# Attention in an encoder block: value products directly behind the next unit's transposes in TensorE's order, the dense products behind them

## The chip, the cores and the metric

The kernel runs on one core of one Trainium2 chip. The metric is the device time of one execution in microseconds (us). Before the change it is 1884.78 us, the median of three runs (1884.11 to 1885.09 us).

## The reference

One layer of a bidirectional encoder runs over two request groups (2048 and 512 tokens, width 1024), each with 16 learned meta tokens in front. Cut to what matters:

```
u = rms_norm(h, norm_g)
qa, ka, va, za, qb, kb, vb, zb, ga, gb = split(u @ w_in)
o_a = neighbourhood_attention(qa, ka, va, na_rpb)   # 8 heads of 64, 8 x 16 token window, plus meta tokens
o_b = window_attention(qb, kb, vb, t5_bias, sink)   # 8 query heads, 2 key heads, +-128 tokens, meta tokens, sink
y_a = (o_a * silu(za)) @ w_proj_a
y_b = (o_b * silu(zb)) @ w_proj_b
h = h + (sigmoid(ga) * y_a + sigmoid(gb) * y_b) @ w_out
out = rms_norm(h without meta tokens, final_g)
```

All is fp32 in the reference. In the kernel an operand of a matmul is split into a high part (rounded to fp32r) and a low part (the rest), and a product is made of three matmuls, or two where one side is narrow.

## The kernel before, in words

The tokens are cut into five windows of 512 (`w` = 0 to 4). The first part (to about 960 us) makes the input projections and stores q, k, v, z and gates in DRAM. The second part, of which the change is a part, runs attention and the dense rest side by side. Its work is cut into 240 **units**. A window has 32 A units, one for each of 8 heads (`p`, `h`) and 4 column groups (`g`), and then 16 B units (`gh` = 0, 1; query block `n` = 0 to 3; `i` = 0, 1), each for two heads. A unit is a generator (`unit_a`, `unit_b`) with five stages:

1. load: q, k, v, bias by DMA, issued on SyncE (SP).
2. **scores** on TensorE (lines 1117 and 1118, or 1223 and 1224, into `s`), maximum with bias on VectorE (line 1047), exponential on ScalarE (line 1054).
3. normalise: reciprocal (line 1058) and scaling (line 1065 on VectorE, line 1063 on ScalarE).
4. **transposes** of the probabilities on TensorE into `tp` (line 1141, or 1243 and 1246), then the split into `ph` (high, ScalarE, line 1144 or 1250) and `pl` (low, VectorE, line 1145 or 1251). In B units the meta tokens go to `pms` by three small copies: lines 1260 (ScalarE), 1261 (VectorE) and 1262 (ScalarE).
5. **value products** on TensorE into `oa` or `ob` (lines 1156 and 1158, or 1267, 1270 and 1272), which read `ph`, `pl` and `pms`, then `ol` (ScalarE, line 1162 or 1274) and the sum into `y` (VectorE, line 1164 or 1277). Of an A head the column group 0 has no value products of its own; they run with those of group 1. The last unit of a pair of heads also multiplies by `z` (GpSimd) and splits the result for the dense part (line 1071 on ScalarE, 1072 on GpSimd).

The dense part (`phases`: gates, `dense_pa`, `dense_pb`, `dense_out`, `dense_fin`) is a generator too. One of its steps is six matmuls of 128x512 (`mm3` twice, lines 146 to 148). `fill(share)` adds `share` to a running sum and makes one step for each whole number reached: `share` is 1 for most B units and 0.5 for most A units, so a B unit has a dense step in each of its two fills and an A unit one in its second fill. In window 0 the shares differ a little, so that some fills make no step.

The loop at the end of `encoder_block` writes TensorE's order out by hand (`manual_schedule` for PE). In an iteration it makes the loads of unit i + 4, the scores of i + 2, the normalising of i + 1, a fill, the transposes of i, a second fill, and the value products of i - 1. The order of the other engines is set by a scheduler from a modelled timeline of the whole program, so it can shift when TensorE's order does. `ph` and `pl` are one tile each; A units write alternating parts of it, B units alternate between two halves. `oa` and `ob` have one PSUM buffer, `tp` has three, shared with a third of the A scores, `s` two, and the dense results two.

Of the kernel before, what the change touches and what calls it, by code (L numbers as in the profile page):

```python
# [95 lines left out]
def encoder_block(ctx: ExitStack, tc: tile.TileContext, xT, x_end, w_in, w_pa, w_pb, w_o, norm_g, final_g,  # L96
# [44 lines left out]
    def move(out, in_):  # L141
        last_move[0] = nc.sync.dma_start(*(f32(a) if a.dtype == F32R else a for a in (out, in_)))
        return last_move[0]
# [73 lines left out]
    class Weights:  # L217
# [16 lines left out]
        def next(self):  # L234
            i = self.i
            self.i += 1
            self.fetch(i + 2)
            self.split(i + 1)
            return self.wt.pop(i)
# [1256 lines left out]
    def phases(w, br):  # L1496

        if br == "a":
            if w == 0:
                yield from islice(gates, GATES_A)  # L1500
            else:
                yield from dense_pb(w - 1)
                yield from dense_out(w - 1, range(0, 4))
        elif w == 0:
            yield from gates
            open_dense()
            yield from dense_pa(0)
        else:
            yield from dense_out(w - 1, range(4, 8))
            pa = dense_pa(w)  # L1510
            yield from islice(pa, 1)
            yield from with_fill(pa, dense_fin(w - 1))
# [7 lines left out]
    units = []  # L1520
# [31 lines left out]
    with tc.manual_schedule(engines={E.PE}):  # L1552
        N = len(units)
        dense, key, due = iter(()), None, 0.0

        def fill(amount):
            nonlocal due
            due += amount
            while due >= 1 and next(dense, "end") != "end":
                due -= 1  # L1560

        for i in range(1, 4):
            next(units[i][2])
        for _ in islice(gates, GATES_0 - 4):
            pass
        for i in range(2):
            next(units[i][2])
        for _ in islice(gates, 4):
            pass
        vbm = vbm_d.rearrange("m g (h f) -> m g h f", h=2)  # L1570
        for h in range(2):
            for r, part in ((0, 0), (32, 0), (64, 1)):
                move(vms[r + 16 * h : r + 16 * h + 16, :, h], vbm[:, :, part, :])
        next(units[0][2])
        for i in range(N):
            br, w, _, weight = units[i]
            if key != (br, w):
                key, dense = (br, w), chain(dense, phases(w, br))
            if i == N - LAST:
                lo_eng[0] = nc.vector  # L1580
            share = COUNT.get(key, 32) * weight / 32 / 2
            if i + 4 < N:
                next(units[i + 4][2])
            if i + 2 < N:
                next(units[i + 2][2])
            if i + 1 < N:
                next(units[i + 1][2])
            fill(share)
            next(units[i][2])
            if [u[0] for u in units[i + 1 : i + 3]] == ["a", "b"]:  # L1590
                next(units[i + 2][2])
            fill(share)
            if i:
                next(units[i - 1][2])
        fill(2)
        next(units[N - 1][2])
        for _ in dense:
            pass
# [106 lines left out]
```

## Time and profile before

| what | us |
|---|---|
| median of three runs | 1884.78 |
| the profiled execution, its own time | 1881.95 |
| its span, first to last instruction | 1880.0 |
| VectorE busy in the span | 1326.6 |
| ScalarE busy in the span | 1146.9 |
| GpSimd busy in the span | 729.4 |

A row of a timeline has the start in us from the span's start, the duration in us, the engine (PE is TensorE, DVE VectorE, ACT ScalarE, POOL GpSimd), the line of the kernel, the operation, the tiles (out<-in), the shapes, and the count of merged instructions. Matmuls overlap in the pipeline, so the time from one start to the next is what a matmul costs TensorE, and the duration is longer than that. A row of the windows has the stretch, its length, and then the busy time of each engine with its count of instructions, the granted TensorE clock (1.00 is full) and the DMA load. A row of the waits names an engine and an instruction, what it waited for, the sum, how often, and the longest.

### The profile page before, as it was taken

Reading aid. Unit: us, or ns where it says so; the run is one execution under the profiler, and the core shown is the slowest. Engines: PE = TensorE matmul, PEld = TensorE weight load, DVE = VectorE, ACT = ScalarE, POOL = GpSimd, SP = SyncE. Lnnn points to the kernel's source line nnn. Section 1 sums busy time; section 2 is a strip of 40 time slices with the busy share of each in tenths; the row PEclk is TensorE's granted clock in tenths of the full one; section 3 lists DMA queues with packets and bytes.
Section 4 is the critical chain, followed back from the end, with each engine's and each line's share of the span. In section 5 each row is a group of like instructions: output and inputs, shape, how many; then the busy total and the mean of one; then the engine's idle time right before and its main releaser. Section 6 shows DMA issues by size and latency. Waiting matters only on the chain.

```text
span 1880.0 us, 29819 instructions
## 1 busy us (share of the span) xinstructions
PE 1857.8 (99%) x9797; PEld 1584.9 (84%) x9797; DVE 1326.6 (71%) x2961; ACT 1146.9 (61%) x2528; POOL 729.4 (39%) x558
## 2 busy tenths in 40 slices
PE   8999999999999999999999999999999999999998
PEld 6988888888888888888878888888888888888887
DVE  8885657556477565444457888878887887888874
ACT  6454444434465443444456797797889788878932
POOL 2005343222202322232323435656844764684420
PEclk9999999999999999999999999999999999999999
DMA  7575666555295677744359878977995996698473
GB/s 262 193 197 187 189 188 183 200 193 184 78 330 197 188 209 208 201 145 150 113 186 320 270 230 264 300 218 243 324 284 178 321 315 225 221 314 261 115 298 132
DMA packets 288145, 414.35 MB, mean 220 GB/s; under 512 B 117736, under 2 KB 162360, under 8 KB 286456
## 3 DMA queue, kind: packets, MB, share of 16 engines
q1 hardware_dynamic: 287704, 412.45, 68.4%
q8 instruction: 78, 1.28, 0.3%
q14 instruction: 75, 0.61, 0.1%
q10 hardware_dynamic: 288, 0.01, 0.0%
HBM read 303.46 MB, written 108.91 MB: 219 GB/s over the span
## 4 chain that ended last, share of the span: by engine, by line
PE 83%; ACT 5%; DVE 5%; DMA 4%; issue 1%; SPq 1%; POOL 1%; ACTq 0%; DVEq 0%
PE pa L850 23%; PE pe L850 11%; PE pc L850 6%; PE mm L148 3%; PE mm L147 3%; PE mm L146 3%; PE tp L1141 3%; PE pso L148 2%; PE psb L148 2%; PE pso L146 2%; PE psb L146 2%; PE pso L147 2%; PE psb L147 2%; PE psa L146 2%; PE psa L148 2%; PE psa L147 2%
## 5 line engine op out<-in xcount | busy, mean ns | idle before, releaser
L208 POOL TENSOR_TENSOR wt<-wraw,wt 128x512 fp32r<-128x512 f32 x164 | 213.0, 1317 | 270.0 <-ACT wt L207 269.9
L850 PE MATMUL pa<-u,wt 128*128 128x512 f32 x1008 | 244.3, 391 | 2.1 <-ACT wt L207 1.1
L850 PE MATMUL pa<-u,x 128*128 128x512 f32 x984 | 236.7, 389 | 0.5 <-ACT u L861 0.5
L850 PEld LDWEIGHTS pa<-u,wt 128*128 128x128 f32 x1008 | 189.9, 189 | 42.4 <-ACT wt L207 1.5
L207 ACT CAST wt<-wraw 128x512 fp32r<-128x512 f32 x312 | 177.9, 619 | 74.7 <-DMA wraw<-in_w_in_dram 27.4
L850 PEld LDWEIGHTS pa<-u,x 128*128 128x128 f32 x984 | 184.5, 188 | 39.3 <-ACT u L861 0.9
L821 POOL TENSOR_TENSOR s<-wraw,raw 128x512 f32<-128x512 f32 x40 | 58.2, 1456 | 278.8 <-DVE x L208 278.8
L146 PE MATMUL mm<-u,wt 128*128 128x512 f32 (+2 forms) x416 | 150.3, 361 | 7.0 <-ACT u L334 7.0
L816 POOL TENSOR_TENSOR s<-raw 128x512 f32<-128x512 f32 x40 | 58.7, 1467 | 234.7 <-DMA raw<-in_w_in_dram 233.2
L147 PE MATMUL mm<-u,wt 128*128 128x512 f32 (+2 forms) x416 | 146.8, 353 | 1.1 <-DVE u L335 1.0
L148 PE MATMUL mm<-u,wt 128*128 128x512 f32 (+2 forms) x416 | 146.8, 353 | 0.1
L208 DVE TENSOR_TENSOR wt<-wraw,wt 128x512 fp32r<-128x512 f32 x148 | 104.7, 745 | 53.8 <-ACT wt L207 53.7
L850 PE MATMUL pe<-u,wt 128*128 128x512 f32 x504 | 121.4, 390 | 0.0
L850 PE MATMUL pc<-u,wt 128*128 128x512 f32 x504 | 121.1, 389 | 0.0
L850 PE MATMUL pe<-u,x 128*128 128x512 f32 x480 | 115.3, 389 | 0.0
L850 PEld LDWEIGHTS pc<-u,wt 128*128 128x128 f32 x504 | 94.6, 188 | 19.6
L850 PEld LDWEIGHTS pe<-u,wt 128*128 128x128 f32 x504 | 94.4, 188 | 19.6
L1144 ACT CAST ph<-tp 128x384 fp32r<-128x384 f32 (+6 forms) x160 | 81.7, 511 | 44.9 <-PE tp L1141 43.5
L1047 DVE CUSTOM_DVE_ANT_0 s<-s,ba 128x384 f32<-128x384 f32 (+5 forms) x160 | 86.9, 544 | 30.6 <-PE s L1118 27.7
L1145 DVE TENSOR_TENSOR pl<-tp,ph 128x384 fp32r<-128x384 f32 (+6 forms) x160 | 94.9, 593 | 18.0 <-ACT ph L1144 15.2
L146 PE MATMUL pso<-mh,wt 128*128 128x512 f32 x256 | 107.1, 418 | 0.0
L829 POOL TENSOR_TENSOR s<-wraw,s 128x512 f32<-128x512 f32 x40 | 53.7, 1343 | 136.2 <-DVE wt L208 135.6
(258 smaller groups left out, 5030.1 us busy)
## 6 DMA issues: line engine op xcount, KB each, us to landing
wraw<-in_w_in_dram SPq DMA_DIRECT2D x86, 512.0 KB
raw<-in_w_in_dram SPq DMA_DIRECT2D x40, 512.0 KB
q<-qa SPq DMA_DIRECT2D x40, 512.0 KB
wraw<-in_w_o_dram SPq DMA_DIRECT2D x32, 512.0 KB
kbt<-kb SPq DMA_DIRECT2D x32, 384.0 KB
qa<-evq SPq DMA_DIRECT2D x20, 512.0 KB
qb<-evq SPq DMA_DIRECT2D x20, 512.0 KB
ka<-evk SPq DMA_DIRECT2D x20, 512.0 KB
```

The costliest lines, as they stand in the source:

```text
L146: nc.tensor.matmul(ps, wh, uh, start=first, stop=False)
L147: nc.tensor.matmul(ps, wh, ul, start=False, stop=False)
L148: nc.tensor.matmul(ps, wl, uh, start=False, stop=last)
L207: nc.scalar.copy(h, r)
L208: low[0] = (eng or lo_eng[0]).tensor_sub(l, r, f32(h)).ins
L816: eng.tensor_add(s1, a21, a22)
L821: eng.tensor_sub(s3, a11, a21)
L850: nc.tensor.matmul(ps, wt[:, a, s], u[:, b, kk, :], start=first and kk == 0 and i == 0, stop=kk == 3 and i == 2, skip_group_check=True)
L1047: nc.vector.tensor_tensor_reduce(s[:, :n], s[:, :n], bias, -1.0, 3.0e38, ALU.add, ALU.min, nm)
L1141: nc.tensor.transpose(tp[:kb, i * P : (i + 1) * P], pr[:, x : x + kb], ident)
L1144: nc.scalar.copy(ph_[:kb, a], tb)
L1145: nc.vector.tensor_sub(pl_[:kb, a], tb, f32(ph_[:kb, a]))
```

## The change

The step of the value products of unit i - 1 moves up in an iteration, from behind the second fill to directly behind the transposes of unit i. The dense step of the second fill follows behind them.

```
@@ -1587,11 +1587,11 @@
                 next(units[i + 1][2])
             fill(share)
             next(units[i][2])
+            if i:
+                next(units[i - 1][2])
             if [u[0] for u in units[i + 1 : i + 3]] == ["a", "b"]:
                 next(units[i + 2][2])
             fill(share)
-            if i:
-                next(units[i - 1][2])
         fill(2)
         next(units[N - 1][2])
         for _ in dense:
```

TensorE's queue before, from the last transposes of B unit n = 2, i = 0, gh = 0 of window 2 (1409.42 us in the profile) to the value products of the unit before it:

```order
L1243 MATMUL tp<-ident,prs 128x128 x6
L1246 MATMUL tp<-ident,prs 32x128
L146 MATMUL pso<-mh,wt 128x512
L147 MATMUL pso<-ml,wt 128x512
L148 MATMUL pso<-mh,wt 128x512
L146 MATMUL pso<-mh,wt 128x512
L147 MATMUL pso<-ml,wt 128x512
L148 MATMUL pso<-mh,wt 128x512
L1267 MATMUL ob<-ph,vb 128x256
L1272 MATMUL ob<-pl,vb 64x256
```

The same place of TensorE's queue in the changed kernel:

```order
L1243 MATMUL tp<-ident,prs 128x128 x6
L1246 MATMUL tp<-ident,prs 32x128
L1267 MATMUL ob<-ph,vb 128x256
L1272 MATMUL ob<-pl,vb 64x256
L1267 MATMUL ob<-ph,vb 128x256
L1272 MATMUL ob<-pl,vb 64x256
L1267 MATMUL ob<-ph,vb 128x256
L1270 MATMUL ob<-pms_8530,vms 64x128 x2
L1272 MATMUL ob<-pl,vb 64x256
L146 MATMUL pso<-mh,wt 128x512
L147 MATMUL pso<-ml,wt 128x512
L148 MATMUL pso<-mh,wt 128x512
```

The eight value matmuls have moved ahead of one dense step of six matmuls; behind that step the scores of the next unit follow as they did.

ScalarE's queue before at the same B unit, from the copy of its transposes to `ph` (L1250) to the last copy of its meta tokens (L1262); the exponentials (L1054) are those of the unit three further on:

```order
L1250 CAST ph<-tp 128x512
L1250 CAST ph<-tp 128x256
L1367 ACTIVATE xres<-hT 128x512
L1063 ACTIVATE prs<-prs,rd 128x402
L1274 COPY ol<-ob 64x256
L1368 ACTIVATE hT<-hT,fg 128x512
L1260 CAST pms_8529<-tp 32x128
L1054 ACTIVATE prs,sm<-s,nm 128x402 x2
L1262 CAST pms_8529<-pms_8529 32x128
```

The same place of ScalarE's queue in the changed kernel:

```order
L1250 CAST ph<-tp 128x512
L1250 CAST ph<-tp 128x256
L1367 ACTIVATE xres<-hT 128x512
L1063 ACTIVATE prs<-prs,rd 128x402
L1274 COPY ol<-ob 64x256
L1368 ACTIVATE hT<-hT,fg 128x512
L1260 CAST pms_8529<-tp 32x128
L1054 ACTIVATE prs,sm<-s,nm 128x402
L1262 CAST pms_8529<-pms_8529 32x128
L1054 ACTIVATE prs,sm<-s,nm 128x402
```

The last copy of the meta tokens has moved ahead of one of the two exponentials.

More of the change, by code (lines that the diff above doesn't have):

```diff
@@ L1589, in encoder_block @@
             next(units[i][2])
+            if i:
+                next(units[i - 1][2])
             if [u[0] for u in units[i + 1 : i + 3]] == ["a", "b"]:
@@ L1592, in encoder_block @@
             fill(share)
-            if i:
-                next(units[i - 1][2])
         fill(2)
```

## The prediction, made before the changed kernel ran

> **What bounds the kernel now.** I read the page's busy times and the chain first, then the windows around the part that the change touches, then TensorE's waits there, and last the timeline at single units.
>
> ```profile
> PE 1857.8 (99%) x9797; PEld 1584.9 (84%) x9797; DVE 1326.6 (71%) x2961; ACT 1146.9 (61%) x2528; POOL 729.4 (39%) x558
> PE 83%; ACT 5%; DVE 5%; DMA 4%; issue 1%; SPq 1%; POOL 1%; ACTq 0%; DVEq 0%
> ```
>
> TensorE is busy 99% of the span and holds 83% of the chain that ended last. The share of a whole span hides stages, so the windows of the attention part follow.
>
> ```profile
> 985.00:1390.00 405.00, 403.50 (x2435) 351.70 (x2433) 330.35 (x950) 321.69 (x820) 216.06 (x171) 1.00 0.87 274
> 1390.00:1800.00 410.00, 408.98 (x2498) 359.90 (x2497) 336.52 (x937) 341.58 (x848) 240.85 (x190) 1.00 0.76 240
> 1800.00:1880.00 80.00, 72.25 (x341) 60.22 (x339) 44.86 (x104) 19.91 (x41) 4.60 (x3) 0.97 0.58 226
> ```
>
> From 985 to 1800 us TensorE is idle for 405 - 403.50 + 410 - 408.98 = 2.5 us in all, at the full clock. VectorE and ScalarE are busy 82 to 83% of the second window: they follow TensorE, with some queueing.
>
> ```profile
> PE fin_v L170 <- DVE pms L1261: 0.5, 2, 0.3
> PE ob L1267 <- DVE y L1277: 0.5, 1, 0.5
> PE fin_v L170 <- POOL ssq L1372: 0.3, 1, 0.3
> ```
>
> These are three of TensorE's five waits there; not one is for `ph` or `pl`. So the change can hardly save anything: it removes no work, and no more than 2.5 us of idle time is there to be saved. What it can do is bring waits in.
>
> **The change, part by part.** Nothing is removed or added. The value step moves up past one dense step. It issues its matmuls, `ol` on ScalarE, the sum into `y` on VectorE and, at the end of a pair of heads, a product and a difference on GpSimd and a copy on ScalarE; it issues no DMA. The loads that SP issues keep their place in the loop, but their buffers come free one dense step earlier, which can only help them. Two prices decide: what the matmuls cost beside their new neighbours, and what cover the value products lose.
>
> ```profile
> 1246.75 0.39 PE L146 MATMUL pso<-mh,wt 128*128 128x512 f32 x1
> 1248.12 0.82 PE L1243 MATMUL tp<-ident,prs 128*128 128x128 f32 x6
> 1248.77 0.27 PE L1246 MATMUL tp<-ident,prs 128*32 128x128 f32 x1
> 1248.80 0.49 PE L146 MATMUL pso<-mh,wt 128*128 128x512 f32 x1
> ```
>
> A dense step costs TensorE 1248.12 - 1246.75 = 1.37 us. Behind a last transpose a dense matmul starts after 0.03 us. Some units of window 0, whose fill made no step, already have value products behind transposes:
>
> ```profile
> 1004.58 0.49 PE L1141 MATMUL tp<-ident,pr 128*128 128x128 f32 x3
> 1004.82 0.43 PE L1156 MATMUL oa<-ph,v 128*128 128x256 f32 x2
> ```
>
> Six transposes take 1248.77 - 1248.12 = 0.65 us, 0.11 each, so the last of these three starts at 1004.80 and the value product 0.02 to 0.03 us behind it, as the dense one does. The new neighbours cost **nothing**.
>
> The cover is worth more. Between the transposes of a unit and its value products there stood a round of the loop and one dense step; now there is the round alone. `ph`, `pl` and `pms` must be ready 1.37 us earlier. A typical A unit (column group 1, window 2):
>
> ```profile
> 1349.24 0.69 DVE L1145 TENSOR_TENSOR pl<-tp,ph 128x512 fp32r<-128x512 f32 x1
> 1351.30 0.34 PE L1156 MATMUL oa<-ph,v 128*128 128x256 f32 x2
> 1351.48 0.35 PE L1158 MATMUL oa<-pl,v 128*64 128x128 f32 x2
> ```
>
> `pl` is ready at 1349.93, the product that reads it starts 1.55 us later, so 0.18 us of margin is left. I went through all 200 units with value products in this way, each operand against the product that reads it. Leaving out the units that have no dense step to lose, the last unit, and the four where the sums of `dense_fin` stand in the step, 26 units have an operand ready less than 1.37 us ahead; the shortfalls add up to 14.4 us (9 A units 2.5, 17 B units 11.9). The first and the last of the 26:
>
> ```profile
> 999.14 0.42 DVE L1145 TENSOR_TENSOR pl<-tp,ph 128x256 fp32r<-128x256 f32 x1 [1.14 <-ACT ph L1144]
> 1000.87 0.35 PE L1158 MATMUL oa<-pl,v 128*64 128x128 f32 x2
> 1788.88 0.28 DVE L1261 TENSOR_TENSOR pms<-tp,pms 32x128 fp32r<-32x128 f32 x1
> 1790.31 0.28 PE L1270 MATMUL ob<-pms,vms 96*64 96x128 f32 x2
> ```
>
> The first lacks 1.37 - (1000.87 - 999.56) = 0.06 us, the last 1.37 - (1790.31 - 1789.16) = 0.22 us. **14.4 us** is the upper end if nothing else moved; **zero** is the lower one, if the two other engines make up all of it. Two things shrink the sum. Neighbouring units (within 5.1 us) share one delay, and a wait for the first gives the second its time: counting the larger alone takes off 0.2 in A and 1.6 in B. And the queues change. Seven B units owe 2.8 us to `pms` standing behind two exponentials:
>
> ```profile
> 1414.74 0.58 ACT L1054 ACTIVATE prs<-s,nm 128x402 f32<-128x402 f32 x1
> 1415.33 0.57 ACT L1054 ACTIVATE prs<-s,nm 128x402 f32<-128x402 f32 x1
> 1416.01 0.30 ACT L1262 CAST pms<-pms 32x128 fp32r<-32x128 f32 x1
> 1417.23 0.28 PE L1270 MATMUL ob<-pms,vms 96*64 96x128 f32 x2
> ```
>
> Here the copy ends 0.92 us ahead, 0.45 short. In ScalarE's new queue it stands behind one exponential, 1416.01 - 1415.33 = 0.68 us earlier, and the shortfall is gone; so for all seven. Two more B units lose a copy (L1071) ahead of theirs.
>
> ```profile
> L1071 ACT CAST yb<-y x20: 602/621/637, 1110.2 to 1803.5; 128x512 fp32r<-128x512 f32 x20
> ```
>
> At its median of 621 ns that is 1.2 us for the two. 14.4 - 1.8 - 2.8 - 1.2 = **8.6 us** is left, made of large and small ones. I take the large ones (over 0.7 us) whose operand stands in the changed queues behind the same work as before, two in A and three in B:
>
> ```profile
> 1007.58 0.56 DVE L1145 TENSOR_TENSOR pl<-tp,ph 128x384 fp32r<-128x384 f32 x1 [0.27 <-ACT ph L1144]
> 1008.64 0.28 PE L1158 MATMUL oa<-pl,v 128*64 128x256 f32 x1
> 1087.11 0.28 DVE L1261 TENSOR_TENSOR pms<-tp,pms 32x128 fp32r<-32x128 f32 x1
> 1087.72 0.28 PE L1270 MATMUL ob<-pms,vms 96*64 96x128 f32 x2
> 1308.61 0.69 DVE L1145 TENSOR_TENSOR pl<-tp,ph 128x512 fp32r<-128x512 f32 x1 [1.12 <-ACT ph L1144]
> 1309.96 0.35 PE L1158 MATMUL oa<-pl,v 128*64 128x128 f32 x2
> 1731.33 0.30 ACT L1262 CAST pms<-pms 32x128 fp32r<-32x128 f32 x1
> 1732.19 0.28 PE L1270 MATMUL ob<-pms,vms 96*64 96x128 f32 x2
> 1769.45 0.30 ACT L1262 CAST pms<-pms 32x128 fp32r<-32x128 f32 x1
> 1770.15 0.28 PE L1270 MATMUL ob<-pms,vms 96*64 96x128 f32 x2
> ```
>
> Their shortfalls are 0.87, 1.04, 0.71, 0.81 and 0.97: **4.4 us**. Small ones I take as made up. The four steps with sums I take at zero: their own waits (0.5 and 0.3 us in the rows above) lie behind the value products now and can shrink, and some of the units there fall short by about as much. Behind a waiting value product stand the dense step, the next scores and the next transposes, so each wait lengthens TensorE's queue, and with TensorE as the bound the end moves by as much.
>
> One large shortfall, 1.1 us at 1291 us, I leave out, because what made it late need not come again:
>
> ```profile
> 1283.70 0.16 DVE L163 SCALAR_TENSOR_TENSOR rs<-rs,rs 128x4 f32<-128x4 f32 x1
> 1286.08 1.22 DVE L163 SCALAR_TENSOR_TENSOR rs<-rs,rs 128x4 f32<-128x4 f32 x1
> 1284.73 2.54 POOL L208 TENSOR_TENSOR wt<-wraw,wt 128x512 fp32r<-128x512 f32 x2 [6.26 <-ACT wt L207]
> ```
>
> A line that takes 0.16 us took 1.22 beside a GpSimd pair that ends at 1287.27, three hundredths ahead of it. The Trainium skill, page "SBUF — State Buffer", section "Who interferes with whom", has a VectorE instruction with both inputs in SBUF wait for the whole of a GpSimd instruction that reads SBUF; the rows agree. By that rule the wait falls where the two queues happen to meet, and if they meet there again the sum is 5.5 us instead of 4.4.
>
> The profiled execution took 1881.95 us, 2.8 below the median of the three runs; it becomes 1886.4, and the median 1884.78 + 4.4 = **1889.2 us**.
>
> **Rivals.** *All hidden.* The sum into `y` now comes before the maxima in many places of VectorE's queue, each wait of TensorE gives the others time, and both have 17% of their time free. Then 0 to 2 us come on top: 1884.8 to 1886.8, no change. It decides whether in those five places an operand comes within one round of the loop. For it: most of the 200 units have cover to spare. Against: the five lack most of a microsecond with the same work ahead.
>
> *Chained waits.* If the reordered queues give back what they gain, the full 14.4 us comes: up to 1899.2. It decides at the margin of about 0.2 us of the A units of group 1, 32 of them in windows 1 to 4. For it: VectorE in places takes a maximum ahead of the reciprocal now. Against: ahead of those `pl` the work is the same.
>
> *Faster.* All 2.5 us of idle time go, and the last window, idle for 7.75 us, loses about 1.8 more because GpSimd or ScalarE ends sooner: 1880.5. The place is the three waits above and the tail. Against: the tail's order is unchanged.
>
> That the change does not do what it says can be excluded by the order of TensorE's queue.
>
> **How the numbers follow.** Forecast (waits of 2 to 8.6 us, 1886.8 to 1893.4): 0.55. Hidden: 0.22. Chained, 8.6 to 14.4 us and over: 0.17. Faster: 0.06. A measurement of this kernel can tell about 0.2%, 3.8 us, from no change; of the forecast's 0.55 some 0.15 lies below that. So faster 0.06, same 0.22 + 0.15 = 0.37, slower 0.40 + 0.17 = 0.57. The range reaches from 1884.0 (hidden, with the runs' own spread) to 1896.5, into the chained case; what is left out is the faster case and about half of the chained one, 0.15.
>
> **What would show it.** TensorE's waits between 985 and 1800 us should name `pl` (line 1145) before line 1158 and `pms` (lines 1261, 1262) before line 1270, with 3 to 9 us in all, none above 1.5; its idle time there should grow from 2.5 to 6 to 9 us; the dense step and the transposes should keep 1.37 and 0.65 us; the window to 985 us should not change. No such waits and the same time mean that the work is hidden; waits in every A head mean that the margin of 0.2 us was not there. I would be wrong altogether if matmuls beside new neighbours ran slower or faster with no wait shown.

## The result and the profile after

| kernel | median, us | range of five runs | ratio to before, 95% interval |
|---|---|---|---|
| before | 1884.11 | 1883.30 to 1885.09 | |
| changed | 1894.87 | 1894.16 to 1897.55 | 1.0061 [1.0049, 1.0072] |

The change makes the kernel 10.8 us slower, 0.6%, more than the 0.2% that a measurement can tell from no change. The forecast was 1889.2 us, a loss of 4.4: the direction and the mechanism hold, the size is less than half of what came. The profiled executions differ by 12.9 us (1894.87 after, 1881.95 before), since the one of before lies 2.2 below its median.

The busy times and the chain of the changed kernel:

```profile
PE 1862.9 (98%) x9797; PEld 1585.5 (84%) x9797; DVE 1332.7 (70%) x2961; ACT 1144.7 (60%) x2528; POOL 729.4 (39%) x558
PE 77%; ACT 9%; DVE 6%; issue 3%; DMA 2%; POOL 2%; SPq 0%; ACTq 0%; DVEq 0%; POOLq 0%
```

The instructions are the same in number. TensorE's part of the chain falls from 83 to 77%, and ScalarE's rises from 5 to 9%: the chain now passes through the engines that TensorE waits for. The windows (stretch, length, busy time of each engine, clock, DMA) show where:

```profile
985.00:1390.00 405.00, 397.04 (x2383) 343.69 (x2382) 326.42 (x926) 313.24 (x800) 214.87 (x170) 1.00 0.84 267
1390.00:1800.00 410.00, 407.54 (x2465) 356.38 (x2464) 336.02 (x936) 341.36 (x850) 233.93 (x185) 1.00 0.76 241
```

TensorE is idle for 405 - 397.04 + 410 - 407.54 = 10.4 us instead of 2.5, and its clock is full in both. The waits behind it, from TensorE's waits between 985 and 1812 us (total, times, longest):

```profile
PE ob L1270 <- ACT pms L1262: 2.1, 5, 0.6
PE s L1223 <- ACT prs L1054: 2.0, 2, 1.3
PE ob L1267 <- ACT prs L1054: 1.9, 2, 1.0
PE oa L1158 <- DVE pl L1145: 1.1, 4, 0.3
PE ob L1267 <- DVE y L1277: 0.9, 2, 0.5
PE s L1117 <- DMA kd<-kam: 0.9, 1, 0.9
PE ob L1270 <- DVE pms L1261: 0.8, 2, 0.6
PE tp L1141 <- DVE pr L1065: 0.4, 1, 0.4
```

`pl` and `pms`, which the forecast named, are there, and with them waits that it did not have. One name is wrong: a first value product (line 1267) does not read the result of an exponential. The rows of such a place, at 1087 us:

```profile
1087.36 0.37 ACT L1274 COPY ol<-ob 64x256 f32<-64x256 f32 x1
1088.13 0.57 DVE L1047 CUSTOM_DVE_ANT_0 s<-s,bb 128x402 f32<-128x402 f32 x1
1088.62 0.57 DVE L1277 TENSOR_TENSOR y<-ob,ol 64x128 f32<-64x128 f32 x2
1089.30 0.29 ACT L1262 CAST pms<-pms 32x128 fp32r<-32x128 f32 x1
1089.34 0.36 PE L1267 MATMUL ob<-ph,vb 128*128 128x256 f32 x1 [0.95 <-ACT prs L1054]
```

A semaphore is a counter that one engine raises when an instruction is done and that another engine waits for. By the program's semaphores this product waits for `ol` and for the sum into `y` of the unit before it, which empty the one buffer of `ob`. `ol` ended at 1087.73; the sum stood behind a maximum on VectorE and ended at 1089.19, and the product started 0.15 us later. The profile names the event that came last, and that was an exponential which nothing there waited for.

So I set the semaphores of every value product against the ends in the trace of after: which of the instructions that it waits for ended last, and how late that made it. Done so, the value steps lose 14.2 us, **14.0** of it in 28 units that lose more than 0.1. (The idle time in the windows is smaller, because a matmul's modelled end lies behind the start of the next one: at 1089.34 the start comes 1.20 us late, and 0.95 of it is shown as idle.) The scores of window 0 that wait for `s` add 1.6 us to the 0.8 of before, a late load of `kd` 0.8. Together with the units' own spacing this agrees: from first transposes to first transposes the loop has become 15.8 us longer, and the stretch ahead of it was 2.75 us shorter in that execution. The same spacing by groups, in us against the one trace of before, for the changed kernel and for some experiments below:

| window and kind | changed | only A moved | only B moved | not window 0 | last copy on GpSimd | meta tokens earlier |
|---|---|---|---|---|---|---|
| 0, A | 4.07 | 3.58 | 0.19 | 0.41 | 4.25 | 4.08 |
| 0, B | 3.49 | 1.27 | 5.65 | 0.02 | 3.67 | 8.34 |
| 1 to 4, A | 1.40 | 5.31 | 1.91 | 0.72 | 0.06 | 3.95 |
| 1 to 4, B | 6.85 | 0.44 | 7.20 | 7.02 | 23.62 | 4.69 |

### The profile page after: what moved, and what is told of

The parts are those of the page before. It is cut to its first block, busy times and chain, and to the rows that moved or that the text cites. A ratio compares the mean times of both kernels' runs of the same rounds, so it can differ in the third digit from the quotient of the medians.

```text
span 1893.0 us, 29842 instructions
## 1 busy us (share of the span) xinstructions
PE 1862.9 (98%) x9797; PEld 1585.5 (84%) x9797; DVE 1332.7 (70%) x2961; ACT 1144.7 (60%) x2528; POOL 729.4 (39%) x558
## 4 chain that ended last, share of the span: by engine, by line
PE 77%; ACT 9%; DVE 6%; issue 3%; DMA 2%; POOL 2%; SPq 0%; ACTq 0%; DVEq 0%; POOLq 0%
PE pa L850 23%; PE pe L850 12%; PE pc L850 6%; PE mm L146 3%; PE mm L147 3%; PE mm L148 3%; PE tp L1141 3%; ACT prs L1054 2%; PE psb L146 2%; PE psb L148 2%; PE psb L147 2%; PE pso L146 2%; PE pso L148 2%; PE oa L1158 2%; PE pso L147 2%
## 5 line engine op out<-in xcount | busy, mean ns | idle before, releaser
L1054 ACT ACTIVATE prs<-s,nm 128x402 f32<-128x402 f32 (+1 forms) x160 | 91.0, 572 | 33.9 <-DVE nm L1047 24.9
L1054 ACT ACTIVATE s<-s,nm 128x384 f32<-128x384 f32 (+5 forms) x160 | 87.0, 544 | 36.1 <-DVE nm L1047 32.1
```

Of the source, the lines that this page charges most:

```text
L1054: nc.scalar.activation(out, s, AF.Exp, bias=nm, scale=-1.0, accum_out=sm)
```

## The experiments

**Parts of the change.** Three kernels move the value step for some units only; the rest keep the old place behind the second fill. The edit of the first, the others with `== "b"` and with `units[i - 1][1] > 0` (the window) in place of the condition:

```diff
             next(units[i][2])
-            if i:
+            if i and units[i - 1][0] == "a":
                 next(units[i - 1][2])
...
             fill(share)
+            if i and not (units[i - 1][0] == "a"):
+                next(units[i - 1][2])
```

A units only:

> Value products moved up for A units alone, B units as before. Cover theory (each value product waits at its own place, because its operands or its PSUM buffer are not ready one dense step earlier): the places add up, so the stretch from the first transposes to the last ones in the profile grows by the A units' share of the change, 4.1 us in window 0 and 1.4 in windows 1 to 4, 5.5 us in all, and the median by 3 to 6 us. Rival (the scheduler's new order of the other engines' queues costs the time, wherever the value products stand): no sum by place, either about nothing or about the whole 10.8 us.

B units only:

> Value products moved up for B units alone, A units as before. Cover theory: the B units' share, 3.5 us in window 0 and 6.9 in windows 1 to 4, 10.3 us from the first to the last transposes, the median up by 6 to 10 us. Rival (queue order): about nothing or about the whole 10.8 us.

All but window 0:

> Value products moved up in windows 1 to 4, window 0 as before. Cover theory: 1.4 us of A and 6.9 of B, 8.3 us from the first to the last transposes; window 0 as in the kernel before, so 7.6 us of the change gone; the median up by 4 to 8 us. Rival (window 0's share is a delay of the loads or queues that is only shifted): the later windows lose more, and the sum stays near the whole.

Measured: 1.0018 [1.0008, 1.0028], 1.0056 [1.0041, 1.007] and 1.0033 [1.002, 1.0045]. The two kinds add up to 0.74%, near the 0.61% of both together, and B carries most of it. Window 0 carries 0.61 - 0.33 = 0.28%, close to half of the loss, in a fifth of the units. The table shows that it does so in place: with window 0 left alone, its two groups lose 0.4 us together, and the B groups of the other windows lose what they lost before. The medians, 3.7, 9.1 and 5.2 us up, lie in the ranges expected. The stretch from first to last transposes grew by 10.7, 15.0 and 8.3 us in the traces, where 5.5, 10.3 and 8.3 were expected: the first two miss. With A alone the A groups of windows 2 and 3 lose 2.9 and 2.7 us, of it 1.1 and 1.4 at transposes that wait for `pr` and 0.7 and 0.8 at a late load of `kd`; in the same groups the full change has 0.5 us of the first and none of the second. With B alone one place in window 0 costs 3.7 us instead of 1.1, and a load of `kbt` in window 3 is 1.9 us late. The schedulers' queues differ from one kernel to the next, and a microsecond or two goes with them.

**Half of the cover.** The dense generators hand out half a step, and the value step stands in the middle of the second fill's step:

```diff
-            fill(share)
+            owed = fill(share, True)
             if i:
                 next(units[i - 1][2])
+            for _ in range(owed):
+                next(dense, None)
```

> Value products in the middle of the dense step of the second fill, behind three of its six matmuls, so that half of the cover (0.69 us) is back. Cover theory with a threshold: of the shortfalls read from the profile before, only those of operands ready less than 0.69 us ahead are left, 3 us in all, so the median is up by 1 to 4 us over before. Rival (cost in proportion to the cover taken away, as with a delay at every unit): half of the change, 5 to 8 us.

Measured: 1.0019 [1.0008, 1.003], 1888.34 us beside 1886.19 before. Half of the cover given back removes two thirds of the loss. The loss follows the cover as shortfalls do, of which the small ones vanish first.

**The last copy of the meta tokens, taken from the transposes.** `pms` is written by three copies; the third (line 1262) waited for the first. Taken from `tp` it waits for the transpose alone. A second kernel gives the B units the two halves of one `ob` tile in turn, a third has both edits, a fourth both in the old order:

```diff
-                    nc.scalar.copy(pm[64:96], f32(pm[0:32]))
+                    nc.scalar.copy(pm[64:96], tm)
```
```diff
-        o = ps_o.tile([P, WTOK], F32, tag="o", name="ob")
+        if ("o", w) not in acc:
+            acc["o", w] = ps_o.tile([P, WTOK], F32, tag="o", name="ob")
+        x = 2 * P * ((2 * n + i) % 2)
+        o = acc["o", w][:, x : x + 2 * P]
```

> The change, with the second copy of the meta tokens (line 1262) made from the PSUM tile instead of from the first copy, so that ScalarE need not wait for its own first copy and the scheduler can put both side by side ahead of the exponentials. Cover theory, operands: TensorE's waits for that copy (2.1 us at 5 places in the changed kernel) go, and 2 to 3.5 us from the first to the last transposes with them; the other places stay. Rival (the wait is for VectorE's part of the meta tokens or for something else at the same place): the waits stay and carry another name, nothing gained.

> The change, with the value products of B units writing the two halves of one PSUM bank in turn, so that a unit need not wait for the sums of the unit before it. Buffer theory (the waits at the first value product, put down to the exponentials and to y, 2.8 us at 4 places, are for ob to be emptied: the sums into y stand behind the maxima in VectorE's queue and did not move up with the value products): those waits go, and 2.5 to 4 us from the first to the last transposes, most of them in window 0. Rival (they are waits for ph, or for ScalarE to come round, as the name of the wait says): the same places wait as long.

> The change with both: meta copy from PSUM and two halves of the bank. If operands and buffer are all that B units wait for: B's share falls from 10.3 to under 4 us, A's 5.5 stay, so the median is up by 3 to 7 us over before instead of 10.8. Rival (a value product that waits no longer here only uncovers the next late operand, the low part pl, at the same unit): B keeps over 7 us and the median stays 8 us or more above before.

> The kernel before with both edits. Cover theory: with a dense step of cover these waits were hidden, so nothing is gained: within 1 us of before from the first to the last transposes, the median within 2 us. Rival (the edits lighten ScalarE and VectorE by themselves, whatever the place of the value products): 3 us or more faster than before.

Measured: 1.0087 [1.0074, 1.0101], 1.0065 [1.0052, 1.0079], 1.0088 [1.0074, 1.0102], 1.0029 [1.0019, 1.0039]. The first expectation fell: the copy came later, not earlier. Freed from the first copy, it has two exponentials between it and the first copy in 26 units of 80, where the changed kernel has 9, and it ended 1.49 us behind the first copy on average instead of 0.78. In the old order it held `tp` as well, and the sums of `dense_fin` (line 170) waited 6.1 us for it in four places. The second tells nothing about the buffer: the semaphores of that kernel still make each first value product wait for the sum into `y` of the unit just before it, since the halves belong to one tile; the same places waited as long.

**The buffer `ob`, in two other ways.** In the first kernel ScalarE copies both halves of `ob` out, so the next unit's products no longer wait for VectorE. In the second the next maximum in program order is queued on VectorE behind the sum, without a wait on data:

```diff
-        ol = at.tile([64, WTOK], F32, tag="ol", name="ol", bufs=1)[:, : 2 * P]
-        nc.scalar.copy(ol, o[64:128, : 2 * P])
+        ol = at.tile([64, WTOK], F32, tag="ol", name="ol", bufs=1)
+        nc.scalar.copy(ol[:, : 2 * P], o[64:128, : 2 * P])
+        nc.scalar.copy(ol[:, 2 * P :], o[:64, : 2 * P])
...
-            nc.vector.tensor_add(y32[hs, qs], o[:64, h * P : (h + 1) * P], ol[:, h * P : (h + 1) * P])
+            nc.vector.tensor_add(y32[hs, qs], ol[:, (2 + h) * P : (3 + h) * P], ol[:, h * P : (h + 1) * P])
```
```diff
+        with ExitStack() as st:
+            if ylast:
+                st.enter_context(tc.issue_after(ylast.pop("i").ins))
             nc.vector.tensor_tensor_reduce(s[:, :n], s[:, :n], bias, -1.0, 3.0e38, ALU.add, ALU.min, nm)
...
-            nc.vector.tensor_add(y32[hs, qs], o[:64, h * P : (h + 1) * P], ol[:, h * P : (h + 1) * P])
+            ylast["i"] = nc.vector.tensor_add(y32[hs, qs], o[:64, h * P : (h + 1) * P], ol[:, h * P : (h + 1) * P])
```

> The changed kernel with one edit: ScalarE copies both halves of ob to SBUF (two copies of 64x256 instead of one) and VectorE adds the two copies, so ob is free when ScalarE is done and the first value product of a B unit no longer waits for the sum into y. By the semaphores of the changed kernel the eleven longest waits of a first value product in B units, 5.7 us together, end with that sum (line 1277), which in ten of the eleven places stands behind other VectorE work while ol was ready 1 to 2.5 us before. Theory (the buffer ob is one term of the loss, beside the late operands): those waits go, and 4 to 5.5 of the 10.8 us with them; the 80 extra copies of 0.37 us on ScalarE put the last pms copy behind two exponentials in 19 units instead of 9, which gives back 1 to 4. So +6 to +9 us against the kernel before, ratio 1.0032 to 1.0048. Rival (each wait is only replaced by that for the next operand): 1.0055 to 1.0075.

> The changed kernel with one edit: the next maximum that is made in program order is queued on VectorE behind the sum into y of a B unit (an order of issue, no new wait on data); no work is added. Theory (ob is emptied late because the sum stands behind maxima and splits in VectorE's queue): of the 5.7 us of waits that end with the sum, 3 to 5 go; +6 to +8 us against the kernel before, ratio 1.0032 to 1.0042. Rival 1 (the maxima held back make the exponentials and with them s late by as much): 1.0055 to 1.0075. Rival 2 (the waits are for the operands in truth, the sum being only the last of several): no wait for the sum, the same time as the changed kernel, 1.005 to 1.0065.

Measured: 1.0209 [1.0193, 1.0225] and 1.0077 [1.0062, 1.0091], the first far above every range that was expected, the second just above them. In the first the wait for the sum is gone, as meant, but the waits for `pms` are many times what they were:

```profile
PE ob L1270 <- ACT pms L1262: 10.1, 15, 1.4
PE ob L1270 <- DVE pms L1261: 7.6, 8, 1.1
PE tp L1243 <- DVE pms L1261: 3.5, 3, 1.2
```

The edit brought two loads of its own. ScalarE has 80 more copies of 0.37 us, 29 us. And the sum, now with both inputs in SBUF, has these durations by its line (least, median and longest, in ns):

```profile
L1278 DVE TENSOR_TENSOR y<-ol x160: 270/285/1422, 1085.2 to 1843.9; 64x128 f32<-64x128 f32 x160
```

The median is that of the changed kernel, 285 against 283 ns, but 37 of the 160 take over 0.4 us and 26.5 us more together; with one input in PSUM none took over 285 ns. All 37 overlap a GpSimd instruction, of the other 123 six do; in the changed kernel 72 of the sums overlap one and none is longer for it. So this run does not price the buffer. The second adds no work and says more. The waits for `pms` take the place of those for the sum; with its lines four further on than in the changed kernel:

```profile
PE ob L1274 <- DVE pms L1265: 3.5, 8, 0.6
PE ob L1271 <- DVE y L1281: 2.8, 4, 1.9
```

By the semaphores the waits that end with the sum fall only from 5.7 to 4.7 us, those for `pms` rise from 4.8 to 6.3. The trace of the changed kernel already says why, if the ends on the other engines are held fixed: were the sum never late, 11.7 of the 14.2 us in its value steps would remain, because behind the sum `pms` is late too (1089.59 in the rows at 1087 us above); were `pms` never late, 10.2; were `pl` never late, 10.4; were the sum and `pms` both never late, 4.8. Each of the two hides the other.

**`pms` on another engine, and earlier.** GpSimd makes the last copy; or the meta tokens are transposed behind the first key block instead of the last:

```diff
-                    nc.scalar.copy(pm[64:96], f32(pm[0:32]))
+                    nc.gpsimd.tensor_copy(pm[64:96], f32(pm[0:32]))
```
```diff
-        slots = [("k", j) for j in range(nbk)] + [("m", 0)]
+        slots = [("k", 0), ("m", 0)] + [("k", j) for j in range(1, nbk)]
...
-                x = slice(c0 + 2 * half, c0 + 2 * half + 2 * nk)
+                x = slice(c0 + half, c0 + half + 2 * nk)
...
-                    x = slice(c0 + 2 * (half + m), c0 + 2 * (half + m) + 2)
+                    x = slice(c0 + 2 * j, c0 + 2 * j + 2)
```

> The changed kernel with one edit: the last copy of the meta tokens (line 1262) is made by GpSimd instead of ScalarE, so it no longer stands behind exponentials. By the semaphores of the changed kernel ten meta products wait for pms, 4.8 us together, 3.1 of it for this copy. Theory (late pms is a term of its own): 2 to 3.5 us go, +7 to +9 us, ratio 1.0037 to 1.0048, if GpSimd takes the copy within 1 us. Rival (GpSimd's queue, where one instruction often takes 1.27 us, makes the copy later than ScalarE did): waits before line 1270 grow and the time is above that of the changed kernel, ratio 1.0065 to 1.012.

> The changed kernel with one edit: a B unit transposes its meta tokens behind its first key block instead of behind its last, so the three copies into pms (lines 1260 to 1262) come ahead of the split of the later blocks; the number of instructions is the same, and the last copy stands behind two exponentials in no unit any more. Worked out from the trace of the changed kernel with the ends of the other engines held fixed, the waits inside the value steps are 14.2 us; 7.9 are left if pms is never late, 11.4 if pl is never late, 12.2 if the sum into y is never late (behind that wait pms is late as well). Theory (pms is the largest term): about 6 us go, and 0 to 2 come back because the later blocks' ph and pl are split later: +4.5 to +7 us against the kernel before, ratio 1.0024 to 1.0037. Rival 1 (the engines' queues only pass the lateness on, to pl of the later blocks or to the sum): 1.005 to 1.0065, with waits before line 1272 or 1267 in place of those before 1270. Rival 2 (pms matters little, the buffer ob does): waits before line 1267 stay at 5 to 6 us and the time within 2 us of the changed kernel, 1.005 to 1.0065, without such new waits.

Measured: 1.0181 [1.0167, 1.0195] and 1.0083 [1.0069, 1.0097], both slower than the changed kernel and above the ranges of the rivals that they speak for. The second expectation also started from a wrong figure: 7.9 us cannot be left without late `pms`, since the waits for `pms` are 4.8 of the 14.2; with 10.2 left some 4 us could go, and not 6. The places say more than the medians. With the copy on GpSimd, the B groups of windows 1 to 3 lose 6.45, 7.55 and 7.46 us, and a single place in each, the wait and the half clock behind it, accounts for 6.71, 7.35 and 7.25 of it. Without it they lose -0.26, 0.20 and 0.21, where the changed kernel loses 1.77, 1.09 and 1.10. The place of window 1:

```profile
1303.66 2.54 POOL L208 TENSOR_TENSOR wt<-wraw,wt 128x512 fp32r<-128x512 f32 x2
1306.13 4.95 POOL L1386 TENSOR_TENSOR hT<-hT,rbs 128x512 f32<-128x512 f32 x4
1311.15 0.52 POOL L1262 CAST pms<-pms 32x128 fp32r<-32x128 f32 x2
1311.49 0.47 PE L1270 MATMUL ob<-pms,vms 96*64 96x128 f32 x2 [4.77 <-POOL pms L1262]
```

Two units' copies stand behind six GpSimd instructions of 1.25 us. Everywhere else in these windows a copy that stands behind no exponential leaves next to no loss. In windows 2 and 3 late `pms` is thus the loss of the B units. In window 1 most of the changed kernel's loss is the 1.14 us at 1291 us, where VectorE's part of `pms` was late (point 7 of the next section). In windows 0 and 4 the B groups still lose 3.7 and 2.2 us with the copy on GpSimd, so `pms` is not the whole there.

The other kernel, with the meta tokens earlier, also takes the loss of the B groups in windows 2 and 3 to 0.11 us each. It gives that back in one place of window 0 (4.86 us more than the changed kernel) and in A groups (2.13 us more in window 3, of it 1.2 at transposes that wait for `pr`). My expectation was wrong on one point: the 16 units with two key blocks now split `ph` and `pl` in two pieces, 16 more instructions on each of two engines. The place in window 0:

```profile
1125.51 0.36 PE L1267 MATMUL ob<-ph,vb 128*128 128x256 f32 x1 [0.98 <-ACT prs L1054]
...
1127.74 0.47 PE L1270 MATMUL ob<-pms,vms 96*64 96x128 f32 x2 [1.64 <-ACT pms L1262]
1128.02 0.41 PE L1272 MATMUL ob<-pl,vb 128*64 128x256 f32 x1
1128.23 0.63 PE L146 MATMUL psa<-ya,wt 128*128 128x512 f32 x1
1128.65 0.63 PE L147 MATMUL psa<-ya,wt 128*128 128x512 f32 x1
1129.08 0.63 PE L148 MATMUL psa<-ya,wt 128*128 128x512 f32 x1
```

After the second wait dense matmuls start 0.42 us apart instead of 0.23. That is the clock, and it is taken up in the last section. No kernel here beats the one before.

## Why the prediction was right in direction, and small

1. *TensorE is the bound, and 2.5 us of idle is all that could be saved.* Right: none of the moved kernels is faster, and where waits came, the end moved with them.
2. *The new neighbours cost nothing.* Right. Where operands are ready, the value step follows its transposes after 0.03 us (the median of the B units), as a dense step did, and the clock of the two windows is full. The loss lies in waits.
3. *Cover of 1.37 us is lost, and 26 units fall short, 14.4 us together.* In the traces this sum, with nothing taken off it, is what came: 14.0 us in value steps. Part of that is luck, since 10.0 of it came in units that were short and 4.0 in units that were not. And the traces as a whole lie 12.9 us apart and the medians 10.8, because the stretch ahead of the loop happened to be 2.75 us shorter and the trace of before is one of its faster executions; the 8.6 us that stood ahead of the choice of the large ones are nearer to the medians. Half of the cover cost a third.
4. *14.4 - 1.8 - 2.8 - 1.2, and of the rest only the five large ones, 4.4 us; "small ones I take as made up".* **This step failed.** The five measured 0.53, 1.11, 0, 0.81 and 0.74 us for the 0.87, 1.04, 0.71, 0.81 and 0.97 of the forecast, 3.2 for 4.4: the sizes are near, though at 1087 us and in part at two others the wait is for the sum into `y`, which I had not counted (point 8). But eleven other units that were short, one of them the last of the loop, waited another 6.8 us, and 13 units that lacked nothing before waited 4.0. The queues did make up some shortfalls and the reasons were sound one by one: of the seven units relieved of an exponential, two waited 0.3 us and five not at all. What I left out is that queues which shift also make something late that was not: another order does it, and so does the place where two engines meet. An example; before, a product of column group 2 in window 0 had 0.05 us more than it needed once the dense step was gone (`pl` ends at 1017.43, and line 1158 reads it at 1018.85, 1.42 later); after, the split starts 0.92 us behind the copy to `ph` instead of 0.48, and the product is late:

```profile
1015.13 0.76 DVE L291 TENSOR_SCALAR eva<-eva 128x512 f32<-128x512 f32 x1
1016.88 0.55 DVE L1145 TENSOR_TENSOR pl<-tp,ph 128x384 fp32r<-128x384 f32 x1
1018.85 0.28 PE L1158 MATMUL oa<-pl,v 128*64 128x256 f32 x1
```
```profile
1012.84 2.54 POOL L208 TENSOR_TENSOR wt<-wraw,wt 128x512 fp32r<-128x512 f32 x2 [0.56 <-ACT wt L207]
1014.37 1.29 DVE L291 TENSOR_SCALAR eva<-eva 128x512 f32<-128x512 f32 x1 [0.75 <-ACT eva L290]
1016.04 0.53 DVE L1145 TENSOR_TENSOR pl<-tp,ph 128x384 fp32r<-128x384 f32 x1
1016.62 0.34 PE L1158 MATMUL oa<-pl,v 128*64 128x256 f32 x1 [0.26 <-DVE pl L1145]
```

The first three rows are of before, the others of after: there `pl` ends at 1016.57, 0.57 us behind the start of the step. VectorE's order did not do this: it has no more ahead of the split than before, and a scaling (line 1065) less. Line 291, ahead of a maximum and a reciprocal, took 1.29 us instead of 0.76 and ended 0.28 us behind the GpSimd pair beside it (1015.38); 12 of its 15 rows in this part of the trace end 0.28 to 0.29 us behind the GpSimd instruction in which they began. With 0.76 us there, `pl` would have been ready at about 1016.04 (an estimate), in time for the product. The product at 1058 us is late in the same way.

5. *Two units lose a copy (L1071) ahead of theirs, 1.2 us for the two.* Too much: their shortfall of 1.21 us each became 0.81 and 0.78, not 0.6. In the rows of the first, the last copy of `pms` still stands behind two exponentials:

```profile
1442.91 0.59 ACT L1054 ACTIVATE prs<-s,nm 128x402 f32<-128x402 f32 x1
1443.49 0.57 ACT L1054 ACTIVATE prs<-s,nm 128x402 f32<-128x402 f32 x1
1444.18 0.29 ACT L1262 CAST pms<-pms 32x128 fp32r<-32x128 f32 x1
1444.53 0.34 PE L1270 MATMUL ob<-pms,vms 96*64 96x128 f32 x2 [0.55 <-ACT pms L1262]
```

6. *The four steps with sums at zero.* Right as a sum: their units wait 0.7 and 0.2 us, two not at all, and the waits of before at line 170, 0.8 us, are gone.
7. *1.1 us at 1291 us "need not come again".* It came again, 1.14 us. A row of line 163 took 1.26 us and the next, line 177, 1.75, beside a GpSimd pair of 2.73:

```profile
1290.66 1.26 DVE L163 SCALAR_TENSOR_TENSOR rs<-rs,rs 128x4 f32<-128x4 f32 x1
1291.95 1.75 DVE L177 TENSOR_TENSOR rs_dg<-ident,rs 128x512 f32<-128x512 f32 x1
1290.43 2.73 POOL L208 TENSOR_TENSOR wt<-wraw,wt 128x512 fp32r<-128x512 f32 x2 [7.27 <-ACT wt L207]
```

The page "SBUF — State Buffer" of the Trainium skill, section "Who interferes with whom", named in the prediction, gave the rival 5.5 us; it was right here, and the sums with both inputs in SBUF above agree with the page.

8. *What the operands are.* I set `ph`, `pl` and `pms` against the products, and not the buffer `ob`, which the sum into `y` has to empty. For five units that sum alone makes the product late, 1.9 us; elsewhere it hides a late `pms`. Nor did I look at the scores that wait for `s`, 1.6 us more than before, at the turn from A to B in window 0.
9. *Idle time of 6 to 9 us, no wait above 1.5.* 10.4, and the longest shown is 1.3. The A units of group 1, with their margin of 0.18 us, mostly kept it: windows 1 to 4 lose 1.4 us there.

## What to carry to other kernels

When an edit takes a fixed cover from many waits, count every shortfall, and take small ones off the sum only for a reason: reordered queues give and take, and here they took about as much as they gave (14.4 us counted, 14.0 in the traces, 10.8 in the medians). That is one kernel, and no rule. Besides the operands, count the buffer that the moved step writes and who empties it. A copy or sum on an engine's queue is late or early by the queue as well as by what it depends on: freed from a dependence it may be queued later.

## What the runs showed of the hardware

A short gap can be enough to halve TensorE's clock. The windows of the kernel with the meta tokens earlier (the granted clock is the third number from the end):

```profile
1120.00:1126.50 6.50, 4.83 (x32) 3.82 (x29) 5.27 (x17) 6.45 (x19) 4.24 (x4) 1.00 0.88 225
1126.50:1133.00 6.50, 5.26 (x16) 4.48 (x17) 4.23 (x13) 2.71 (x8) 0.00 (x0) 0.50 0.47 165
1133.00:1140.00 7.00, 7.00 (x46) 6.20 (x45) 4.25 (x16) 5.53 (x17) 2.09 (x2) 0.98 0.42 120
```

Here two starts came 1.25 and 1.92 us behind the ones before them, 2.2 us apart. Of single gaps, four of 2.19 to 2.27 us were each followed by dense matmuls 0.42 to 0.43 us apart instead of 0.23, three of 2.10 us were not. Two gaps of 1.24 and 1.13 us, 1.4 us apart, did it too where only B units moved. So did single gaps of 1.30 and 1.21 us in the kernel with two copies out of `ob`, where eight matmuls of 128x1 (line 170, 0.81 us in all) came soon behind the gap. These are cases, and no threshold follows from them. In this part of the program the changed kernel has no gap above 1.6 us and no slow stretch, so its loss is waits alone; the experiments whose gaps halved the clock paid twice. The page "TensorE: Matmul & The Clock Gate" of the Trainium skill, Part 1, has the clock fall to half after an idle window of about 3.4 us; these runs show it after less.
